# Output projection of the last head but one, moved into the tail of the last head

## The chip, the cores and the metric

The kernel runs on one core of a Trainium2 chip. TensorE (PE) multiplies and writes to PSUM; PEld is its weight load. VectorE (DVE), ScalarE (ACT) and GpSimd (POOL) do the element-wise work, SyncE (SP) issues most transfers, and POOL issues transfers that add to what is in SBUF. The metric is the device time of one execution in microseconds (us), lower is better. The profile shows one execution.

## The reference

One inference step of a two-layer decoder in fp32: 512 prompt tokens and 8 x 4 sample tokens (544 columns), model width 1024. Each layer is a mixer and a gated FFN. Layer 0 mixes by a short convolution, layer 1 by retention with 4 heads. What matters here is the retention mixer and the swiglu behind it:

```python
def swiglu(x, w_gate, w_up, w_down):
    return (jax.nn.silu(x @ w_gate) * (x @ w_up)) @ w_down
...
    z = x @ w_in
    q, k, v, g = jnp.split(z, [QK_DIM, 2 * QK_DIM, 2 * QK_DIM + V_DIM], axis=-1)
...
    o, S = retention_chunkwise(q, k, v, s0)
    of = o.astype(jnp.float32)
    mu = jnp.mean(of, axis=-1, keepdims=True)
    var = jnp.mean(jnp.square(of - mu), axis=-1, keepdims=True)
    of = (of - mu) * lax.rsqrt(var + GN_EPS)
    of = of.transpose(0, 2, 1, 3).reshape(B, L, V_DIM) * gn_g.astype(jnp.float32)
    out = (jax.nn.silu(g) * of.astype(x.dtype)) @ w_out
...
        x = x + m
        x = x + swiglu(rmsnorm(x, norm_ffn[i]), ffn_w_gate[i], ffn_w_up[i], ffn_w_down[i])
```

`retention_chunkwise` gives, per head, causal scores within the new tokens, the part that comes from the state `s0`, and the new state. The sample tokens have a state per sequence of 256 x 512 per head (read and written), the prompt starts at zero.

## The kernel before

**Products.** Activations are held transposed: `x[k]` is a 128 x 544 tile of 128 model features, in two halves of 272 columns. Every fp32 operand is split into a high and a low part (`xh`, `xl`; `wh`, `wl`), and a product is three passes: high x high, high x low, low x high. `project` (L165-180) does this for one 128-column block of weights: per k-tile three passes over two halves, so 48 matmuls for 8 k-tiles and 24 for 4. `split` (L187-190) makes the parts: ACT copies the high part, DVE subtracts. `split_adding` (L192-196) makes the low part without DVE: ACT copies twice and POOL issues a load that adds the weights in memory onto the negated high part. `load_piece` (L133) loads a weight block on SP (`w`) and splits it; `w`, `wh` and `wl` have three buffers each. `residual` (L265-271) adds a product from PSUM to `x` on DVE.

**PSUM.** `psum()` gives a wide tile of two banks, tag `mm`, of which there are two; `bank()` gives single banks, tag `sm`, four of them. A new tile waits until the readers of the old tile in its buffer are done. `wide(...)` (L66) sets which kinds `psum()` takes in turn.

**Order.** The program is written for the engines together; a planner in the framework orders each engine's queue, and `tc.issue_after` pins some instructions behind others. Tiles of one tag share buffers in turn.

**Stages.** The convolution mixer, FFN 0 (from about 155 us), the retention mixer head by head (L1166-1231), FFN 1 (from about 1080 us), the final norm. The FFN's gate and up products use a scheme of seven products for eight blocks: `weights7` (L424) forms sums of weight blocks on DVE, `operand` (L573) forms sums of blocks of `x`, and a `Job` runs `product` 1 to 7 (`sm` banks, matmuls at L476). `run` (L511) calls `prepare` (weights of a job), then `begin`, `middle` and `end`, and prepares the next job ahead of `middle`. The gate's `Silu` is at L598. `start` runs one activation of `Copy` at L302 early on, the "warm" one.

**One head.** `value` (L885) projects the values from four weight pieces (`rtv`), and in its middle splits the rotated queries and keys (`qk_split`, L878), forms the sample scores and transposes the keys. Then come four gate projections (`gate_project`, L994: 48 matmuls, DVE multiplies by the norm, ACT applies Silu and a scale), the prompt's state (L958) and the scores (L1010). The tail interleaves, for the four blocks of 128 prompt tokens and the four sample states:

- `sample_outputs` (L1100): products of sample queries and a state S; `i` = 0 begins with L1106,
- `states_update` (L1113): four matmuls at L1124 into two wide tiles, DVE adds them to S in two halves (L1129), SP stores S (L1130); `states_load` (L1095) loads the next S on SP,
- `inner` (L1042): the scores times values for one token block,
- `normalized` (L1030): statistics on DVE (L1035, L1036), a power on POOL (L223), `yn` on DVE (L1039),
- `gated` (L1059): four transposes of `yn` on PE, and DVE multiplies the gate tile by them (L1066, for the sample tokens L1070).

In heads 0 to 2 the query and key projections of the next head lie among these steps. Then `out_project` (L1132) splits the head's gated output (`yh`, `yl`) and runs eight pieces n = 0 to 7 of 24 matmuls, each with an addition to `x[n]`; the next head follows. In the last head, gate projections 2 and 3 lie in the tail instead, and `out_project` gets `rest`: the left half of pieces 0 and 1 first, before the last block is gated, then the right half; its weights but the first are split by `split_adding`.

Of the kernel before, what the change touches and what calls it, by code (L numbers as in the profile page):

```python
# [47 lines left out]
def hybrid_decode_kernel(ctx: ExitStack, tc: tile.TileContext, a: dict, o: dict):  # L48
# [226 lines left out]
    with ExitStack() as c0:  # L275
# [13 lines left out]
        def start():  # L289
# [221 lines left out]
    def run(jobs, after, steps):  # L511

        jobs[0].lead = True
        jobs[0].prepare()
        jobs[0].begin()
        jobs[0].weave = jobs[1].weave = steps
        for i, job in enumerate(jobs):
            nxt = jobs[i + 1] if i + 1 < len(jobs) else None
            if nxt is not None:
                nxt.prepare()  # L520
            job.middle()
            if nxt is not None:
                nxt.begin()
            job.end()
            after(i)
# [19 lines left out]
    def ffn(layer, next_gain):  # L545
        with ExitStack() as c1:
# [86 lines left out]
            def down(ms, order):  # L633
# [36 lines left out]
            groups = [list(range(m, min(m + GROUP, HJ))) for m in range(0, HJ, GROUP)]  # L670
            jobs = [job for m in range(HJ) for job in gate_up(m)]

# [101 lines left out]
    with ExitStack() as c2:  # L774
# [103 lines left out]
        def qk_split(h, st, which):  # L878
            r = st["rot"][which]
            th = tp.tile([P, 2, SEQ], F32R, tag=f"qkh{which}", name=nm("qkh"), bufs=1)  # L880
            tl = tp.tile([P, 2, SEQ], F32R, tag=f"qkl{which}", name=nm("qkl"), bufs=1)
            split(th, tl, r[:, :, :SEQ])
            st["qk"[which]] = (th, tl)
# [109 lines left out]

        def gate_project(h, st, n, inside=None):  # L994
            if n == 0:
                st["gate"] = tp.tile([P, 4, T], F32, tag="gate", name=nm("gate"), bufs=1)
            wh, wl = load_piece(a["rtg"][h, n], KT * P)
            pt = [bank(), bank()] if inside else psum()
            if inside:
                project(pt, wh, wl, 0, xh, xl, last=False, ks=range(KP))  # L1000
                inside()
                project(pt, wh, wl, 0, xh, xl, first=False, ks=range(KP, KT))
            else:
                project(pt, wh, wl, 0, xh, xl)
            g = halves(st["gate"][:, n, :])
# [53 lines left out]
        def gated(h, st, yn, it, pt=None):  # L1059

            pt = bank() if pt is None else pt
            for n in range(4):
                last_product[0] = nc.tensor.transpose(pt[:, token_tiles(n)], yn[:, token_tiles(n)], ident)
            if it < 4:
                gs = st["gate"][:, :, token_tiles(it)]
                nc.vector.tensor_mul(gs, gs, pt.rearrange("p (n t) -> p n t", n=4))  # L1066
            else:
                gs = st["gate"][:, :, SEQ:].rearrange("p n (g c) -> p n g c", g=4)
                ys = pt.rearrange("p (n g c) -> p n g c", n=4, g=4)[:, :, :, 0:8]
                nc.vector.tensor_mul(gs, gs, ys)  # L1070

# [59 lines left out]

        def out_project(h, st, rest=None):  # L1132
# [6 lines left out]
            def split_gated(c):  # L1139
                for n in range(4):  # L1140
                    split(yh[n][:, c], yl[n][:, c], st["gate"][:, n, c])

            split_gated(slice(0, HT if rest else T))
            wide("m" if rest else "mms")
            for n2 in (0, 2, 1, 3):
                wh, wl = load_piece(a["rtout"][h, n2], 2 * 4 * P, adding=rest is not None and n2 > 0)
                pts = []
                for n in range(2):
                    pts.append(psum())
                    if n2 == 0 and rest:  # L1150
                        rest[n]()
                        project(pts[n], wh, wl, n * 4 * P, yh, yl, hfs=(0,))
                    else:
                        project(pts[n], wh, wl, n * 4 * P, yh, yl)
                        residual(2 * n2 + n, pts[n])
                if n2 == 0 and rest:
                    split_gated(slice(HT, T))
                    for n in range(2):
                        project(pts[n], wh, wl, n * 4 * P, yh, yl, hfs=(1,))
                        residual(n, pts[n])  # L1160
            wide("m")

# [3 lines left out]
        for h in range(NH):  # L1166
# [24 lines left out]
            if more:  # L1191
                nxt = qk_start(h + 1)
                for which in (1, 0):
                    qk_scale(nxt, which)
                with tc.issue_after(last_product[0].ins):
                    qk_project(h + 1, nxt, 1, 0)
                with tc.issue_after(last_product[0].ins):
                    gated_pair(h, st, (yn0, 0), (yn1, 1))
                sample_outputs(h, st, 3)
                p3 = inner(h, st, 3)  # L1200
                yn2 = normalized(p2)
                yns = normalized(st["po"])
                states_update(h, st, 2)

                def inside():
                    states_update(h, st, 3)
                    gated(h, st, yn2, 2)

                qk_project(h + 1, nxt, 1, 1, inside)
                yn3 = normalized(p3)  # L1210
                gated_pair(h, st, (yns, 4), (yn3, 3))
# [3 lines left out]
            else:  # L1215
                yn2 = normalized(p2, "gt")
                gate_project(h, st, 2, lambda: states_update(h, st, 2))

                def inside():
                    sample_outputs(h, st, 3)  # L1220
                    states_update(h, st, 3)

                gate_project(h, st, 3, inside)
                yns = normalized(st["po"], "rot1")
                gated_pair(h, st, (yn0, 0), (yn1, 1))
                gated(h, st, yn2, 2)
                p3 = inner(h, st, 3)
                gated(h, st, yns, 4)
                yn3 = normalized(p3)
                out_project(h, st, [lambda: None, lambda: gated(h, st, yn3, 3)])  # L1230
            st = nxt
    ffn(1, None)


# [114 lines left out]
```

## Time and profile before

| what | value |
|---|---|
| median of 3 runs | 1468.25 us (1466.82 to 1468.54) |
| profiled execution | 1468.62 us, span 1466.40 us |
| mean granted PE clock | 0.996 |
| PE busy | 1449.5 us, 99% of the span |
| DVE busy | 959.4 us, 65% |
| ACT busy | 632.1 us, 43% |
| POOL busy | 130.5 us, 9% |

Times inside the profile count from the span's start. A matmul's record overlaps the next one's, so the spacing of starts, not the length of a record, is what one costs. The chain is followed back from the last instruction to whatever released each step. A stretch's row gives the busy time of each engine in it and the clock that the throttle granted to PE, as a share of full speed: a PE that is busy at clock 0.5 does half the work.

### The profile page before, as it was taken

The page shows a single profiled execution, that of the slowest core. Times are in us where ns is not written, and L with a number is a line of the kernel's source. Part 1 is how long each engine was busy: PE and PEld are TensorE (multiplying, and loading weights), DVE is VectorE, ACT ScalarE, POOL GpSimd, SP SyncE. Part 2 cuts the span into 40 slices and gives each one's busy share as a digit, 9 for nine tenths or more (in the row PEclk, how much of TensorE's full clock was granted, in tenths as well). Part 3 has the DMA queues.
Part 4 walks back from the last instruction along what each step waited for, and adds up shares of the span by engine and source line. Part 5 has one row for each costly group of instructions (what it writes and reads, how often), then busy time and mean ns, then how long its engine had stood idle before and what let it go on. Part 6 is the DMA issues. An engine that isn't in the chain of part 4 may idle for free.

```text
span 1466.4 us, 26224 instructions
## 1 busy us (share of the span) xinstructions
PE 1449.5 (99%) x10920; PEld 1378.7 (94%) x10920; DVE 959.4 (65%) x1489; ACT 632.1 (43%) x925; POOL 130.5 (9%) x171
## 2 busy tenths in 40 slices
PE   9999999999999999999999999999999999999997
PEld 9999999999999999898988978987789999999997
DVE  5644678848748557648546835835698847748655
ACT  5222467626536435241141223214286626526434
POOL 0100011101101003000000000000111101101002
PEclk9999999999999999999999999999999999999999
DMA  6222246635536436237234623713646635536432
GB/s 225 78 95 89 89 104 146 153 109 130 130 108 149 125 73 199 92 115 258 75 124 164 202 81 112 253 53 120 202 113 140 146 115 129 143 106 140 122 80 83
DMA packets 80694, 189.62 MB, mean 129 GB/s; under 512 B 7728, under 2 KB 25008, under 8 KB 80576
## 3 DMA queue, kind: packets, MB, share of 16 engines
q1 hardware_dynamic: 66576, 162.01, 35.2%
q0 software_dynamic: 13136, 24.72, 10.3%
q8 instruction: 85, 1.39, 0.4%
q10 hardware_dynamic: 864, 1.22, 0.2%
q14 instruction: 33, 0.27, 0.1%
HBM read 166.75 MB, written 21.18 MB: 128 GB/s over the span
## 4 chain that ended last, share of the span: by engine, by line
PE 90%; DVE 6%; DMA 1%; ACT 1%; POOL 1%; issue 1%; DVEq 0%; POOLq 0%; ACTq 0%
PE mm L173 37%; PE sm L476 31%; PE sm L173 8%; PE sm L897 2%; PE sm L898 2%; PE sm L899 2%; PE sm L161 1%; PE sm L163 1%; PE sm L162 1%; PE sm L1108 1%; DVE S L1129 1%; DMA w<-in_ffgu_dram 1%; DVE ol L189 1%; DVE wl L189 1%; DMA S<-in_rets_dram 1%
## 5 line engine op out<-in xcount | busy, mean ns | idle before, releaser
L188 ACT ACTIVATE wh<-w 128x1024 fp32r<-128x1024 f32 (+4 forms) x139 | 129.6, 936 | 346.6 <-PE mm L173 223.3
L476 PE MATMUL sm<-oh,wh 128*128 128x272 f32 x704 | 204.2, 290 | 3.1 <-ACT oh L188 1.7
L476 PE MATMUL sm<-ol,wh 128*128 128x272 f32 x704 | 203.5, 289 | 1.1 <-DVE ol L189 1.1
L476 PE MATMUL sm<-oh,wl 128*128 128x272 f32 x704 | 203.3, 289 | 0.2 <-DVE wl L420 0.2
L173 PE MATMUL mm<-xh,wh 128*128 128x272 f32 x932 | 195.3, 290 | 0.0
L173 PE MATMUL mm<-xh,wl 128*128 128x272 f32 x932 | 192.5, 289 | 0.0
L173 PE MATMUL mm<-xl,wh 128*128 128x272 f32 x932 | 192.4, 288 | 0.0
L189 DVE TENSOR_TENSOR wl<-w,wh 128x1024 fp32r<-128x1024 f32 (+4 forms) x139 | 150.2, 1085 | 27.7 <-ACT wh L188 25.4
L269 DVE TENSOR_TENSOR x<-x,mm 128x544 f32<-128x544 f32 x91 | 65.4, 719 | 139.1 <-PE mm L173 139.0
L476 PE MATMUL sm<-oh,h 128*128 128x272 f32 x528 | 152.0, 288 | 0.0
L476 PE MATMUL sm<-oh,l 128*128 128x272 f32 x528 | 151.7, 288 | 0.0
L476 PE MATMUL sm<-ol,h 128*128 128x272 f32 x528 | 151.6, 287 | 0.0
L173 PEld LDWEIGHTS mm<-xh,wh 128*128 128x128 f32 x932 | 146.5, 189 | 4.8 <-DVE wl L189 3.4
L173 PEld LDWEIGHTS mm<-xl,wh 128*128 128x128 f32 x932 | 146.2, 189 | 0.1
L173 PEld LDWEIGHTS mm<-xh,wl 128*128 128x128 f32 x932 | 145.5, 189 | 0.2
L476 PEld LDWEIGHTS sm<-oh,wh 128*128 128x128 f32 x704 | 132.7, 188 | 4.6 <-ACT oh L188 2.3
L476 PEld LDWEIGHTS sm<-ol,wh 128*128 128x128 f32 x704 | 132.8, 189 | 1.5 <-DVE ol L189 1.5
L476 PEld LDWEIGHTS sm<-oh,wl 128*128 128x128 f32 x704 | 133.5, 190 | 0.5 <-DVE wl L420 0.5
L422 POOL DMA_DIRECT2D wl<-in_ffgu_dram x88 | 75.5, 858 | 647.9 <-ACT wl L421 298.3
L419 ACT ACTIVATE wh<-w 128x1024 fp32r<-128x1024 f32 x88 | 93.3, 1060 | 75.0 <-PE sm L476 47.9
L476 PEld LDWEIGHTS sm<-oh,h 128*128 128x128 f32 x528 | 99.4, 188 | 0.2 <-ACT oh L188 0.2
L476 PEld LDWEIGHTS sm<-oh,l 128*128 128x128 f32 x528 | 99.6, 189 | 0.0
(260 smaller groups left out, 3087.3 us busy)
## 6 DMA issues: line engine op xcount, KB each, us to landing
w<-in_ffgu_dram SPq DMA_DIRECT2D x88, 512.0 KB, 4.0
wl<-in_ffgu_dram POOLq DMA_DIRECT2D x88, 256.0 KB, 4.7
w<-in_ffdn_dram SPq DMA_DIRECT2D x96, 192.0 KB, 2.6
S<-in_rets_dram SPq DMA_DIRECT2D x16, 1024.0 KB, 7.6
out_rets_dram<-S SPq DMA_DIRECT2D x16, 1024.0 KB, 5.5
w<-in_cvin_dram SPq DMA_DIRECT2D x21, 512.0 KB, 3.5
w<-in_rtqk_dram SPq DMA_DIRECT2D x16, 512.0 KB, 3.6
w<-in_rtv_dram SPq DMA_DIRECT2D x16, 512.0 KB, 3.6
```

Source lines behind the costliest of these rows:

```text
L161: nc.tensor.matmul(out, lh, rh, start=start, stop=False, skip_group_check=True)
L162: nc.tensor.matmul(out, lh, rl, start=False, stop=False, skip_group_check=True)
L173: last_product[0] = nc.tensor.matmul(half(pt, hf)[:, :HT], w[:, c], act[k][:, hf * HT : (hf + 1) * HT], start=(first and k == ks[0] and i ...
L188: h = nc.scalar.activation(dh, src, AF.Copy)
L189: last_low[0] = nc.vector.tensor_sub(dl, src, dh.bitcast(F32))
L269: last_residual[0] = nc.vector.tensor_add(xk, xk, p)
L419: nc.scalar.activation(wh, w, AF.Copy)
L422: nc.gpsimd.dma_start(wl[:, n:], src[:, n:], accum_op=ALU.add)
L476: last = nc.tensor.matmul(out, w[:, c], b[k][:, at, :], start=(first and k == 0 and i == 0), stop=(k == n - 1 and i == 2), skip_group_chec ...
L897: nc.tensor.matmul(out, xh[kt][:, ts_], wh[:, cw], start=(kt == 0), stop=False)
L898: nc.tensor.matmul(out, xh[kt][:, ts_], wl[:, cw], start=False, stop=False)
L899: nc.tensor.matmul(out, xl[kt][:, ts_], wh[:, cw], start=False, stop=(kt == KT - 1))
```

## The change

- The warm activation is `Silu` instead of `Copy`.
- In both FFNs the jobs are made, and the first one's weights prepared, ahead of the loop that forms the operands.
- `qk_split` puts high and low parts into one tile (tag `qkhl0`, `qkhl1`).
- The last head's gates lie in two tiles of two blocks each (in the buffers of `gt` and `qkhl1`), so the gate tile of head 2 stays alive. `gated` works per tile: two DVE multiplies in the last head where there was one.
- Head 2 no longer runs `out_project`. In the last head, once all gates are projected (as in the other heads, ahead of the first `sample_outputs`), `held_parts` splits head 2's gated output into `xh[0..3]` and `xl[0..3]`, which held x until then. `held_project(n)` is one piece of head 2's output projection with its addition to x. Pieces 4, 5, 2 and 3 stand in the tail where other heads have the next head's query and key projections; piece 5 in single banks.
- Pieces 0, 1 and, later, 6 and 7 of head 2 stay in PSUM without an addition (`held[n]`), and `last_project` adds the last head's product on top of them before one addition to x. Its order is 0, 1, 4, 5, 2, 3, 6, 7; the split by halves (`rest`) is gone; all its weights but the first are made by `split_adding`.

```diff
-                nc.scalar.activation(warm, ones[:, 0:1], AF.Copy)
+                nc.scalar.activation(warm, ones[:, 0:1], AF.Silu)
...
         jobs[0].lead = True
-        jobs[0].prepare()
         jobs[0].begin()
...
+            jobs = [job for m in range(HJ) for job in gate_up(m)]
+            jobs[0].prepare()
             made_in = MADE if layer == 0 else list(range(KT))
...
+            if h == NH - 1 and n % 2 == 0:
+
+                t = tp.tile([P, 2, T], F32, tag=("gt", "qkhl1")[n // 2], name=nm("gate"), bufs=1)
+                st["gate"].append(t)
...
+        def gated_parts(st):
             yhh = vp.tile([P, 4, T], F32R, tag="vyh", name=nm("yh"), bufs=1)
             yll = vp.tile([P, 4, T], F32R, tag="vyl", name=nm("yl"), bufs=1)
             yh = [yhh[:, n, :] for n in range(4)]
             yl = [yll[:, n, :] for n in range(4)]
...
+            for n in range(4):
+                split(yh[n], yl[n], gate_tile(st, n))
+            return yh, yl
...
+        held = {}
+
+        def held_parts(st):
+            for n in range(4):
+                split(xh[n], xl[n], gate_tile(st, n))
+
+        def held_project(n, add=True, single=False):
+
+            if n % 2 == 0:
+                held["w"] = load_piece(a["rtout"][NH - 2, n // 2], 2 * 4 * P)
+            pt = [bank(), bank()] if single else psum()
+            project(pt, *held["w"], n % 2 * 4 * P, xh[:4], xl[:4], last=add)
+            if add:
+                residual(n, pt)
+            else:
+                held[n] = pt
+
+        def last_project(st):
+            y = gated_parts(st)
+            ws = {}
+            for n in (0, 1, 4, 5, 2, 3, 6, 7):
+                if n >= 6:
+                    held_project(n, False)
+                if n % 2 == 0:
+                    w = load_piece(a["rtout"][NH - 1, n // 2], 2 * 4 * P, adding=n > 0)
+                pt = held[n] if n in held else psum()
+                project(pt, *w, n % 2 * 4 * P, *y, first=n not in held)
+                residual(n, pt)
...
-            if more:
-                gate_project(h, st, 2)
-                gate_project(h, st, 3)
+            gate_project(h, st, 2)
+            gate_project(h, st, 3)
+            if not more:
+                held_parts(older)
             sample_outputs(h, st, 0)
...
+            if more:
                 qk_project(h + 1, nxt, 1, 1, inside)
+            else:
+                held_project(5, single=True)
+                inside()
+                held_project(2)
+            yn3 = normalized(p3)
+            if not more:
+                held_project(3)
+            gated_pair(h, st, (yns, 4), (yn3, 3))
+            if more:
                 qk_project(h + 1, nxt, 0, 0)
                 qk_project(h + 1, nxt, 0, 1)
+            if h < NH - 2:
                 out_project(h, st)
...
+            elif not more:
+                held_project(0, False)
+                held_project(1, False)
+                last_project(st)
```

The removed `else` branch held the last head's own order: gate 2 around `states_update` 2, gate 3 around `sample_outputs` 3 and `states_update` 3, then the transposes and `out_project` with `rest`.

More of the change, by code (lines that the diff above doesn't have):

```diff
@@ L1137, in out_project @@
             yl = [yll[:, n, :] for n in range(4)]
[L1139 to L1144, printed above, removed]
+            for n in range(4):
+                split(yh[n], yl[n], gate_tile(st, n))
+            return yh, yl
+        def out_project(h, st):
+            y = gated_parts(st)
+            wide("mms")
             for n2 in (0, 2, 1, 3):
-                wh, wl = load_piece(a["rtout"][h, n2], 2 * 4 * P, adding=rest is not None and n2 > 0)
-                pts = []
+                w = load_piece(a["rtout"][h, n2], 2 * 4 * P)
@@ L1148, in out_project @@
                 for n in range(2):
[L1149 to L1160, printed above, removed]
@@ L1203, in hybrid_decode_kernel @@
[L1203 to L1207, printed above, removed]
[L1209 to L1211 removed]
+                else:
+                    held_project(4)
+            with tc.issue_after(last_product[0].ins):
+                gated_pair(h, st, (yn0, 0), (yn1, 1))
+            sample_outputs(h, st, 3)
@@ L1212, in hybrid_decode_kernel @@
+            gated_pair(h, st, (yns, 4), (yn3, 3))
+            if more:
                 qk_project(h + 1, nxt, 0, 0)
                 qk_project(h + 1, nxt, 0, 1)
+            if h < NH - 2:
                 out_project(h, st)
[L1215 to L1230, printed above, removed]
```

64 lines of the change are left out of this document (35 added, 29 removed).

## The prediction

> **What bounds the kernel now.** I read the page's engine totals first, then the share of each engine in the chain that ended last, then the busy time of each engine by stage (stretch, its length, then busy time of PE, PEld, DVE, ACT and POOL, then the granted clock).
>
> ```profile
> PE 1449.5 (99%) x10920; PEld 1378.7 (94%) x10920; DVE 959.4 (65%) x1489; ACT 632.1 (43%) x925; POOL 130.5 (9%) x171
> ...
> PE 90%; DVE 6%; DMA 1%; ACT 1%; POOL 1%; issue 1%; DVEq 0%; POOLq 0%; ACTq 0%
> ```
>
> ```profile
> 897.00:1005.00 108.00, 107.93 (x744) 93.01 (x743) 65.39 (x99) 27.21 (x35) 3.24 (x5) 1.00 0.42 142
> 1005.00:1105.00 100.00, 94.71 (x660) 83.53 (x660) 75.98 (x131) 53.43 (x84) 11.12 (x14) 0.97 0.53 144
> ```
>
> PE is busy 99% of the span and makes 90% of the chain, so the change, which moves matmuls without adding or removing any, can win only PE's idle time and its slow clock. The stretch from 897 holds head 2, its output projection and the start of head 3: PE idles 0.07 us there. The next holds the rest of head 3 and the entry of the second FFN: PE idles 100 - 94.71 = 5.29 us and the clock averages 0.97. This is what PE waited for there (wait, count, longest), and where it lost time:
>
> ```profile
> PE sm L476 <- ACT oh L188: 1.7, 1, 1.7
> PE mm L173 <- ACT yh L188: 1.2, 1, 1.2
> PE sm L476 <- DVE ol L189: 0.8, 1, 0.8
> PE sm L161 <- DVE yn L1039: 0.4, 1, 0.4
> ```
>
> ```profile
> 1050.00:1052.00 2.00, 1.61 (x12) 1.19 (x10) 2.00 (x4) 0.00 (x0) 0.00 (x0) 1.00 0.90 239
> 1052.00:1054.00 2.00, 1.17 (x7) 0.99 (x8) 1.49 (x6) 1.39 (x4) 0.73 (x1) 1.00 0.81 156
> 1054.00:1056.00 2.00, 1.75 (x10) 1.53 (x9) 1.58 (x4) 0.00 (x0) 0.00 (x0) 0.64 0.54 107
> 1056.00:1058.00 2.00, 2.00 (x11) 2.00 (x11) 0.46 (x1) 0.00 (x0) 0.00 (x0) 0.51 0.00 0
> ...
> 1082.00:1084.00 2.00, 0.54 (x3) 0.30 (x2) 2.00 (x4) 0.87 (x2) 0.00 (x0) 1.00 0.00 0
> 1084.00:1086.00 2.00, 0.68 (x2) 0.42 (x3) 2.00 (x5) 1.40 (x2) 0.14 (x1) 0.82 0.00 0
> 1086.00:1088.00 2.00, 2.00 (x10) 2.00 (x11) 2.00 (x3) 0.98 (x2) 0.71 (x1) 0.50 0.56 133
> 1088.00:1090.00 2.00, 2.00 (x15) 2.00 (x15) 2.00 (x5) 0.85 (x3) 0.00 (x0) 0.83 0.97 236
> ```
>
> Idle is followed by a slow clock. Busy time times what the clock lacked: 1.75 x 0.36 + 2 x 0.49 = 1.6 us at 1054-1058, and 0.68 x 0.18 + 2 x 0.50 + 2 x 0.17 = 1.5 us at 1084-1090. So this stretch loses 5.3 + 3.1 = 8.4 us: nearly all at two places, the output projection's start (its operand's split on ACT) and the FFN's entry (DVE busy throughout, operands late).
>
> A third place lies in the first FFN:
>
> ```profile
> 221.41 1.28 ACT L598 ACT_TABLE_LOAD   x1
> ```
>
> ```profile
> 224.00:226.00 2.00, 1.16 (x10) 0.95 (x9) 2.00 (x3) 1.97 (x4) 0.27 (x1) 1.00 0.07 23
> ```
>
> ACT loads a table, and 0.84 us of PE idle follows, with no slow clock after it. All losses: 8.4 + 0.84 = **9.2 us**, the most that can be won.
>
> **The change, part by part.** The sum is made against the profiled execution: 1468.62 us, its span 1466.40 and 2.22 around it. That is 0.37 above the median of 1468.25, to which I take the result over.
>
> *Warm activation as Silu.* In the built order the load at L598 is gone and the one at the start stays, so the 0.84 us can go. Two ACT operations, not the load alone, stand between the load and PE's next weights; 1.28 off ACT exceeds 0.84, so I take all of it (bounds 0 and 0.84).
>
> *First job's weights prepared ahead of the operand loop.* In the first FFN this shifts a few DVE operations by one or two places around a gap in which DVE waits for a load:
>
> ```profile
> 196.02 0.69 DVE L435 TENSOR_TENSOR w<-w,w 128x512 f32<-128x512 f32 x1 [2.71 <-DMA w<-in_ffgu_dram]
> ```
>
> Two moved operations of 0.7 fit in 2.71: nothing (1.4 without the gap). In the second FFN it counts, below.
>
> *Out-projection of head 2 taken from ahead of head 3.* PE goes from the last query matmuls straight into `value(3)`. What the 24 us covered is the rotation of the queries on DVE and the loads of the value weights.
>
> ```profile
> 949.84 0.72 DVE L865 TENSOR_TENSOR rot<-mm,gt 128x544 f32<-128x544 f32 x1
> ...
> 953.65 0.72 DVE L876 TENSOR_TENSOR rot<-rot,rt 128x544 f32<-128x544 f32 x1
> ```
>
> ```profile
> 973.70 0.39 PE L897 MATMUL sm<-wh,xh 128*128 128x512 f32 x1
> ```
>
> The rotation ends at 954.4. PE would reach its first user 11 us after 949.6 (from 973.70 two weight pieces take until 985), at about 960.9: nothing lost; with that cover gone it would be 4.8. On SP the four value loads take the places of four `rtout` loads; those move behind gates 2 and 3, ahead of the last stores. Nothing lost.
>
> *Gates in two tiles, `held_parts`.* Each gated multiply becomes two halves: 5 more DVE operations, about 0.1 us each beyond the halved width, off PE's path. The eight split operations, 4 on ACT and 4 on DVE of about 0.7 us, lie under gate 3's 6 us and are read 8.8 us after it: nothing.
>
> *Head 3's tail.* The inner products' waits are now filled with held pieces. I time it from T, the start of the first sample output (L1106), with head 2's rows, where the same steps run in this order around a 48-matmul query projection.
>
> ```profile
> 908.98 0.39 PE L1106 MATMUL sm<-vs,scp 128*128 128x512 f32 x1
> ...
> 917.75 0.41 PE L173 MATMUL mm<-xh,wh 128*128 128x272 f32 x2
> ...
> 923.72 0.60 PE L1063 MATMUL mm<-cb,yn 128*128 128x128 f32 x4
> ...
> 925.88 1.04 PE L1108 MATMUL sm<-S,qm 128*8 128x512 f32 x8
> ...
> 928.69 0.51 PE L1124 MATMUL mm<-vs,kns 32*128 32x512 f32 x4
> ```
>
> ```profile
> 913.53 4.30 SPq L1130 DMA_DIRECT2D out_rets_dram<-S  x2
> ...
> 919.72 3.70 SPq L1098 DMA_DIRECT2D S<-in_rets_dram  x2
> ```
>
> ```profile
> S<-in_rets_dram SPq DMA_DIRECT2D x1, 1024.0 KB, 5.9
> ```
>
> ```profile
> S<-in_rets_dram SPq DMA_DIRECT2D x1, 1024.0 KB, 8.6
> ```
>
> Held 4 starts at T+8.8 and, as half of the 5.97 from 917.75 to 923.72, ends at T+11.8. From there to update 2 is 928.69 - 923.72 = 4.97, less sample 3's 0.98, which now comes later: T+15.8. After 0.44 for the update and one matmul, sample 3 is wanted at T+16.35. Its state is loaded at 919.72, T+10.74, and lands 5.9 to 8.6 later (the row of this load, and the slowest): T+16.6 to T+19.3. Wait **0.3** (0 to 3.0; I take this load's own row). Then sample 3, the rest of held 5 (23 x 0.125 = 2.9), update 3 and four transposes: held 2 is wanted at T+21.4. It needs one of the two wide PSUM buffers, which the first half of state update 3 on DVE frees:
>
> ```profile
> 929.46 1.21 DVE L1129 SCALAR_TENSOR_TENSOR S<-S,mm 128x1024 f32<-128x1024 f32 x1
> 930.59 0.80 DVE L1039 TENSOR_SCALAR yn<-sm,mv,rs 128x512 f32<-128x512 f32 x1
> ```
>
> ```profile
> 1027.00 1.42 DVE L1035 BATCH_NORM_STATS2 bst<-sm 128x6 f32<-128x512 f32 x2
> ...
> 1033.30 0.15 DVE L222 TENSOR_SCALAR rs<-mv 128x1 f32<-128x1 f32 x1
> 1034.18 0.81 DVE L1039 TENSOR_SCALAR yn<-sm,mv,rs 128x512 f32<-128x512 f32 x1 [0.72 <-POOL rs L223]
> ```
>
> DVE, in the built order: update 2 starts 0.77 after its matmuls, T+16.55; two halves at 1.13 each (929.46 to 930.59), T+18.8; two statistics, 1.35; small ones, 0.3; 0.88 from `rs` to `yn` by way of POOL; `yn` 0.72; two gate halves 0.7; half of update 3, 1.13: T+23.9. PE waits **2.5** there (0.6 if the statistics, the turn over POOL and the gate halves, 1.9 in all, overlap better; 3.0 at most). Later, held 0 waits for an addition to x: 0.72 less the four transposes ahead of it, **0.5** (0 to 0.7).
>
> *Slow clock.* 1.22 us of idle in 1050-1054 (0.39 + 0.83) was followed by the rates 0.64 and 0.51; 0.84 at 224 was not. A wait of 2.5 is nearer the first: a dip at **1.6**, as at 1054 (0 to 3.1, two dips). [...]
>
> *Start of the last projection.* Head 3's own split, on which PE waited 1.2, now lies under held 0 and 1 (6 us). What is late next is the low part of the weights of pieces 6 and 7. Their buffers come free 4 pieces of 3.01 us after the start of the last projection, P+12.0; two ACT copies and two operations of the FFN's squares ahead of them end at P+14.1 to P+15.8; POOL issues 0.3 later; the landing took
>
> ```profile
> wl<-in_rtout_dram POOLq DMA_DIRECT2D x3, 512.0 KB, 7.0
> ```
>
> ```profile
> wl<-in_rtout_dram POOLq DMA_DIRECT2D x1, 512.0 KB, 5.6
> ```
>
> so P+20.0 to P+23.1, and PE asks at 7 x 3.01 + 0.3 = P+21.4. I take P+22.1, with ACT late and between the landings' ends: **0.7** (0 to 1.7). The earlier pieces have 3 to 4 us to spare.
>
> *Entry of the second FFN.* Four additions to x fall away (1, 0, 6, 7 no longer twice), and the first job's weights are prepared ahead of later operands.
>
> ```profile
> 1060.91 0.72 DVE L269 TENSOR_TENSOR x<-x,mm 128x544 f32<-128x544 f32 x1
> ...
> 1080.52 0.71 DVE L269 TENSOR_TENSOR x<-x,mm 128x544 f32<-128x544 f32 x1
> ```
>
> Before, 19.6 us lay between the first and the last addition for DVE's operand work, which then ran on to 1096 while PE starved. After, pieces 6 and 7 are double: 9 x 3.01 = 27 us of PE for about 26 of DVE, by the built order's operations at their durations. The last operand chain is just in time: **0.3** (0 to 4.9, all that is lost there now with its dip).
>
> **Sum.** New losses: 0.3 + 2.5 + 0.5 + 1.6 + 0.7 + 0.3 = 5.9. Gain 9.2 - 5.9 = 3.3 from 1468.25: **1465.0 us**.
>
> **Rivals.**
> 1. The wait comes without a slow clock: gain 4.9, 1463.4; with DVE running better too, waits of 1 in all, 1460. For it: 0.84 us cost no clock. Against: 1.22 did.
> 2. Little measurable: the state load takes 8.6 (wait 3.0 for 0.3) or a second dip of 1.5 comes; gain 0.6 to 1.8, 1466.5 to 1467.7. For it: the slow landing is in the trace. Against: this load's own row.
> 3. Slower: DVE's service of the two wide PSUM buffers becomes the bound. Each piece of 3.01 us needs one, freed by an addition of 0.72 queued behind state updates of 1.21 and statistics. If five of the ten pieces wait 1.5 (7.5) and two dips follow (3.1) with the 1.8 of other waits, the losses are 12.4: 1471.5. It decides once new losses pass 9.2. Against: DVE's 75.98 busy of 100 leaves room.
>
> **Numbers.** Forecast (1464 to 1466.5) 0.40, of which I put half beyond 0.2%; rival 1 0.30; rival 2 0.12; rival 3 0.18. 0.2% is 2.94 us, about what a measurement of this kernel can tell from no change. Faster: 0.20 + 0.30 = 0.50; same 0.20 + 0.12 = 0.32; slower 0.18. The range 1459.5 to 1471 leaves out half of rival 3 and more, and the last bit of rival 1. The cases of a gain alone: 1459.5 to 1466.5.
>
> **What would show it.** No table load at L598 and PE full at 224. PE's waits from 1005 on: a wide PSUM buffer freed by L1129 around held 2, about 2.5; the accumulated `wl` ahead of pieces 6 and 7, under 2; no 1.7 on `oh` and no clock below 1 at the FFN's entry. I am wrong if PE still idles over 2 us at the entry (DVE work not covered), if `value(3)` waits, or if several PSUM waits on x additions add up.

## The result, and the profile after

The changed kernel takes 1461.33 us (median of 6 runs, 1460.43 to 1463.54) where the kernel before took 1467.74 beside it (6 runs, 1466.82 to 1468.54). The ratio is 0.996, with a 95% interval of 0.9947 to 0.9973: 4.0 to 7.8 us faster. The forecast was 3.3 us faster; the direction and the range hold, the gain is about twice the forecast.

The page of the changed kernel, engine totals and share of the chain:

```profile
PE 1444.1 (99%) x10920; PEld 1374.5 (94%) x10920; DVE 956.2 (66%) x1483; ACT 631.3 (43%) x920; POOL 130.5 (9%) x171
...
PE 92%; DVE 5%; ACT 1%; DMA 1%; POOL 1%; issue 0%; DVEq 0%; SPq 0%; ACTq 0%; POOLq 0%
```

The profiled execution took 1460.43 us, span 1458.4. PE does the same 10920 matmuls in 5.4 us less busy time: busy time contains the slow clock (in the kernel before, 128x272 matmuls start 0.125 us apart at clock 1.00, from 1053.54 to 1054.04, and 0.23 apart at 0.5, from 1055.51 to 1056.87: a little over half the work). By stage (columns as in the prediction; head 2 to the start of the last head's gates, then the tail and the FFN's entry), and the stretches of the tail and the entry in which PE idles:

```profile
897.00:997.00 100.00, 99.93 (x656) 83.55 (x655) 59.57 (x90) 28.53 (x39) 3.24 (x5) 1.00 0.45 151
997.00:1100.00 103.00, 99.28 (x757) 90.94 (x756) 80.09 (x136) 53.91 (x77) 12.03 (x15) 1.00 0.53 143
```

```profile
1024.00:1028.00 4.00, 3.24 (x24) 1.79 (x24) 3.32 (x4) 0.00 (x0) 0.00 (x0) 1.00 0.19 71
1028.00:1032.00 4.00, 2.96 (x24) 2.33 (x23) 3.42 (x10) 1.06 (x1) 1.05 (x2) 1.00 0.69 259
...
1080.00:1084.00 4.00, 2.62 (x19) 2.19 (x18) 4.00 (x8) 2.77 (x6) 0.45 (x1) 1.00 0.54 90
```

Idle in the tail and the entry is 103 - 99.28 = 3.7 us where it was 5.3, and the granted clock is 1.00 throughout, where 3.1 us had gone to a slow clock.

Where the time went can be read from the starts of the FFN's groups of products (L476), between which both kernels run the same number of matmuls. In the first FFN, from its first product to its second group, it is 126.54 us before and 125.20 now. From the last group of the first FFN to the first product of the second, with all of the retention mixer between, it is 553.46 and 550.57. In the second FFN, from its first product to its second group, it is 130.11 and 126.49. These are 1.3, 2.9 and 3.6 us; with 0.2 at the start they are the 8.0 us between the two spans.

What PE waited for from 980 to 1105:

```profile
PE mm L173 <- DVE S L1137: 1.0, 1, 1.0
PE sm L476 <- ACT g L535: 0.9, 1, 0.9
PE sm L1116 <- DMA S<-in_rets_dram: 0.8, 1, 0.8
PE sm L476 <- ACT oh L188: 0.5, 1, 0.5
PE mm L173 <- ACT wh L194: 0.5, 1, 0.5
```

The first is the wait of held piece 2 for the wide buffer, the third the state load ahead of sample output 3 (L1108 before, L1116 now): both were forecast, with other sizes. The last is held piece 0. The copy named is for a later piece, and PE does not read it there: DVE's addition to `x` for piece 3, at 1038.19, which frees the wide buffer that held piece 0 takes, ran to 1038.91, and PE went on at 1039.06. The two with L476 are the FFN's entry.

### The profile page after: what moved, and what is told of

The parts are those of the page before. It is cut to its first block, busy times and chain, and to the rows that moved or that the text cites. A ratio compares the mean times of both kernels' runs of the same rounds, so it can differ in the third digit from the quotient of the medians.

```text
span 1458.4 us, 26223 instructions
## 1 busy us (share of the span) xinstructions
PE 1444.1 (99%) x10920; PEld 1374.5 (94%) x10920; DVE 956.2 (66%) x1483; ACT 631.3 (43%) x920; POOL 130.5 (9%) x171
## 3 DMA queue, kind: packets, MB, share of 16 engines
q0 software_dynamic: 13136, 24.72, 10.2%
q10 hardware_dynamic: 864, 1.22, 0.2%
## 4 chain that ended last, share of the span: by engine, by line
PE 92%; DVE 5%; ACT 1%; DMA 1%; POOL 1%; issue 0%; DVEq 0%; SPq 0%; ACTq 0%; POOLq 0%
PE mm L173 39%; PE sm L476 31%; PE sm L173 7%; PE sm L897 2%; PE sm L898 2%; PE sm L899 2%; PE sm L161 2%; PE sm L163 1%; PE sm L162 1%; DVE S L1137 1%; PE sm L1116 1%; PE mm L904 1%; DVE wl L189 0%; DVE x L269 0%; PE mm L1068 0%
## 5 line engine op out<-in xcount | busy, mean ns | idle before, releaser
L173 PE MATMUL mm<-xh,wh 128*128 128x272 f32 x1020 | 213.1, 290 | 1.6 <-DVE S L1137 1.0
L173 PE MATMUL mm<-xh,wl 128*128 128x272 f32 x1020 | 210.7, 289 | 0.0
L173 PE MATMUL mm<-xl,wh 128*128 128x272 f32 x1020 | 210.0, 287 | 0.1
L476 PE MATMUL sm<-oh,wh 128*128 128x272 f32 x704 | 203.4, 289 | 1.1 <-ACT g L535 0.9
L476 PE MATMUL sm<-ol,wh 128*128 128x272 f32 x704 | 202.8, 288 | 0.0
L476 PE MATMUL sm<-oh,wl 128*128 128x272 f32 x704 | 202.4, 288 | 0.0
L173 PEld LDWEIGHTS mm<-xh,wh 128*128 128x128 f32 x1020 | 159.9, 188 | 7.3 <-DVE wl L189 3.4
L173 PEld LDWEIGHTS mm<-xl,wh 128*128 128x128 f32 x1020 | 159.6, 188 | 0.3 <-DVE xl L201 0.3
L173 PEld LDWEIGHTS mm<-xh,wl 128*128 128x128 f32 x1020 | 159.0, 188 | 0.2
L476 PE MATMUL sm<-oh,h 128*128 128x272 f32 x528 | 152.2, 288 | 0.5 <-ACT oh L188 0.5
L476 PE MATMUL sm<-oh,l 128*128 128x272 f32 x528 | 151.6, 288 | 0.0
L476 PE MATMUL sm<-ol,h 128*128 128x272 f32 x528 | 151.6, 287 | 0.0
L476 PEld LDWEIGHTS sm<-oh,wh 128*128 128x128 f32 x704 | 132.2, 188 | 1.9 <-ACT g L535 1.5
L476 PEld LDWEIGHTS sm<-oh,wl 128*128 128x128 f32 x704 | 132.8, 189 | 0.0
L476 PEld LDWEIGHTS sm<-ol,wh 128*128 128x128 f32 x704 | 132.2, 188 | 0.2 <-DVE ol L189 0.2
L476 PEld LDWEIGHTS sm<-oh,h 128*128 128x128 f32 x528 | 99.4, 188 | 1.1 <-ACT oh L188 0.9
L476 PEld LDWEIGHTS sm<-oh,l 128*128 128x128 f32 x528 | 99.4, 188 | 0.0
```

Source lines behind the costliest of these rows:

```text
L173: last_product[0] = nc.tensor.matmul(half(pt, hf)[:, :HT], w[:, c], act[k][:, hf * HT : (hf + 1) * HT], start=(first and k == ks[0] and i ...
L476: last = nc.tensor.matmul(out, w[:, c], b[k][:, at, :], start=(first and k == 0 and i == 0), stop=(k == n - 1 and i == 2), skip_group_chec ...
```

## Experiments

All ratios are to the kernel before, run beside each on the same chip; the changed kernel has 0.996.

### The warm activation alone

```diff
-                nc.scalar.activation(warm, ones[:, 0:1], AF.Copy)
+                nc.scalar.activation(warm, ones[:, 0:1], AF.Silu)
```

(on the kernel before)

> The kernel before with the warm activation as Silu and nothing else. Theory: the table load in the first FFN goes, and with it the wait of 0.8 us that followed it (the prediction's 0.84): about 1466.9. Rival: between the first FFN's first product and its second group of products the changed kernel took 125.20 us against 126.54, so the load costs more than the wait shown, 1.3 to 1.5 us: about 1466.3. Second rival: what that stretch won came from the early weight preparation, and this kernel stays at 1467.7.

Measured: 1467.32 us, ratio 0.9993 (0.9984 to 1.0001): 1.0 us faster, with an interval from 2.4 faster to 0.2 slower. The trace is clearer than the time. PE at 224 to 226 in this kernel, where it had 1.16 of 2 us and now has all:

```profile
224.00:226.00 2.00, 2.00 (x18) 2.00 (x18) 2.00 (x5) 1.25 (x3) 0.85 (x1) 1.00 0.21 70
```

The wait goes; whether the load is worth 0.8 or 1.4 us the times don't tell. The trace does: from the first product of the first FFN to its second group this kernel takes 125.12 us where the kernel before takes 126.54, so 1.4 us, as the rival had it. This run showed something else, by chance. Around the start of the last output projection it has the same wait as the kernel before, and no slow clock behind it:

```profile
1050.00:1054.00 4.00, 2.56 (x17) 1.90 (x15) 3.48 (x9) 1.39 (x4) 0.73 (x1) 1.00 0.77 156
1054.00:1058.00 4.00, 3.72 (x26) 3.29 (x27) 2.73 (x7) 1.39 (x4) 0.00 (x0) 1.00 0.16 31
```

1.44 us of idle, then clock 1.00; the kernel before had 1.22 us of idle there and then 0.64 and 0.51. The same wait in the same code is followed by a slow clock in one execution and not in another. At the entry of the second FFN it was the other way round: there this execution spent 6.8 us at half clock, and the kernel before 3.4.

### The early weight preparation alone, and the changed kernel without it

```diff
         jobs[0].lead = True
-        jobs[0].prepare()
         jobs[0].begin()
...
+            jobs = [job for m in range(HJ) for job in gate_up(m)]
+            jobs[0].prepare()
             made_in = MADE if layer == 0 else list(range(KT))
```

(on the kernel before; and, the other way round, undone in the changed kernel)

> The kernel before with the first job's weights prepared ahead of the operand loop, in both FFNs, and nothing else. Theory: at the second FFN's entry DVE stays the bound, since the work is only reordered; between 0.5 us slower and 1 us faster. Rival: the early weights are the main gain at that entry; about 3 us faster, 1464.7, with PE's waits at 1080 to 1090 gone.

> The changed kernel with the first job's weights prepared inside run, as before. Theory: the entry of the second FFN is covered by the double pieces 6 and 7 and by the four additions less, so it costs under 1 us: 1461.3 to 1462.3. Rival: early weights carry that entry: about 3 us slower, 1464.3, with a wait of over 2 us and a slow clock there.

Alone on the kernel before: 1473.66 us, ratio 1.0033 (1.0021 to 1.0046), 4.8 us **slower**, which neither theory had. Undone in the changed kernel: 1462.04 us, ratio 0.996 (0.9946 to 0.9973), the same as with it. So the early preparation is no part of the gain of the changed kernel. Alone it does nothing in the first FFN (126.43 us from the first product to the second group, for 126.54); the loss is at the entry of the second, 137.18 for 130.11. The profiled execution is the slowest of the five, at a mean clock of 0.992 where the others have 0.993 to 0.997. Two of PE's waits there, and two stretches:

```profile
PE sm L476 <- DVE ol L189: 1.7, 2, 1.2
...
PE sm L476 <- DVE wl L420: 1.0, 1, 1.0
```

```profile
1088.00:1092.00 4.00, 1.57 (x8) 1.15 (x8) 3.98 (x8) 1.92 (x3) 0.00 (x0) 1.00 0.38 66
1092.00:1106.00 14.00, 13.31 (x61) 12.87 (x60) 5.92 (x11) 4.60 (x10) 2.43 (x2) 0.51 0.32 94
```

DVE is full until 1092 and PE idles 2.4 us: sums of the first job's weights (L436 at 1088.40, L437 at 1090.28) stand in DVE's queue between the low parts of operands (`ol`) that PE waits for, and PE then waits for the low part of those weights (`wl`) as well. Then PE runs at half clock for 14 us, although it hardly waits any more. The slow clock costs more (0.49 x 13.31 = 6.5 us) than the wait that precedes it.

### Held pieces added by themselves

```diff
-                    held_project(n, False)
+                    held_project(n)
...
-                held_project(0, False)
-                held_project(1, False)
+                held_project(0)
+                held_project(1)
```

(on the changed kernel: both edits, then the second alone for pieces 0 and 1, then the first alone for 6 and 7; the matmuls stay the same, and each piece is one more addition to x)

> The changed kernel with pieces 0, 1, 6 and 7 of head 2 added to x by themselves, not held in PSUM: four additions of 0.72 us more on DVE, the same matmuls. Theory: DVE is busy throughout ahead of the second FFN's first product, so what it gets more there PE waits longer: the two additions of pieces 6 and 7 count (1.4 us), those of 0 and 1 lie where DVE is half idle: 1 to 3 us slower, 1462.3 to 1464.3. Rival: DVE catches up: within 0.5 us of the changed kernel. Second rival: the wide PSUM buffers, which must be emptied between the two products of each piece, add waits ahead of the last project too: over 4 us slower.

> The changed kernel with pieces 0 and 1 of head 2 added to x by themselves; 6 and 7 stay in PSUM. Adding all four by themselves cost 6.3 us (1467.68 for 1461.33). Theory: the second FFN's entry is where DVE is the bound and its small waits bring a slow clock behind them; pieces 0 and 1 are added 25 us earlier, where DVE has gaps, so at most 1.5 us: 1461.3 to 1462.8, no clock below 1 at the entry. Rival: the sum of DVE's work counts wherever it is, half of the 6.3: about 1464.5.

> The changed kernel with pieces 6 and 7 of head 2 added to x by themselves; 0 and 1 stay in PSUM. Theory: these two additions (1.4 us of DVE) stand in the queue right ahead of the second FFN's first operands and carry nearly all of the 6.3 us: 1465 to 1468, with half clock of 7 to 11 us behind the entry in the trace. Rival: half, 1464.5, without a slow clock.

Measured: all four 1467.68 us, 0.9996 (0.9987 to 1.0004); 0 and 1 alone 1462.42, 0.9958 (0.9944 to 0.9972); 6 and 7 alone 1467.44, 0.9992 (0.9983 to 1.0001). With all four added by themselves no gain is left that can be measured; that is more than the theory's 1 to 3 us and has the size of the second rival, but not its mechanism, since the waits ahead of the last projection are as in the changed kernel (0.9, 0.9 and 0.5 for 1.0, 0.8 and 0.5). Pieces 0 and 1 cost nothing that can be measured. Pieces 6 and 7, two additions of 0.72 us, carry the whole: 0.0032 of 1468, 4.7 us. In the traces that is in one place: from the first product of the second FFN to its second group 131.61 us with 6 and 7 added by themselves, for 126.49 in the changed kernel; the other two stages differ by 0.2 and 0.4. And it is not the chance of one execution: the mean granted clock is 0.994 to 0.996 in all 11 executions with 6 and 7 added by themselves, and 0.997 to 0.999 in all six of the changed kernel. The waits of the kernel with 6 and 7 added by themselves, and the stretches around the FFN's entry:

```profile
PE sm L476 <- DVE wl L420: 1.3, 1, 1.3
PE mm L173 <- DVE S L1137: 1.1, 1, 1.1
PE sm L476 <- DVE ol L189: 0.8, 1, 0.8
```

```profile
1082.00:1086.00 4.00, 1.52 (x9) 0.87 (x7) 4.00 (x8) 3.66 (x5) 0.00 (x0) 1.00 0.26 45
1086.00:1096.00 10.00, 10.00 (x56) 9.92 (x56) 4.46 (x9) 2.45 (x6) 2.43 (x2) 0.66 0.48 131
```

1.44 us more on a DVE that is full there make PE's idle 2.5 us in four (in the changed kernel 1.4), and a stretch at clock 0.66 over 10 us follows, 3.4 us lost. In the kernel with all four:

```profile
1078.00:1087.00 9.00, 6.13 (x39) 4.98 (x39) 9.00 (x16) 7.45 (x12) 0.85 (x1) 1.00 0.47 86
1087.00:1097.00 10.00, 10.00 (x46) 9.92 (x47) 4.17 (x8) 1.46 (x4) 2.43 (x2) 0.52 0.48 131
```

2.9 us of idle over nine, then 10 us at 0.52. These kernels still have the early preparation, which by itself did harm at a DVE-bound entry. What the two additions would cost without it was not tried.

### A longer wait at held piece 2

```diff
+                more_ops = 1 if h == NH - 1 and i == 3 and w == 0 else 0
-                nc.vector.scalar_tensor_tensor(Si, Si, _gamma(h) ** 4, pu, op0=ALU.mult, op1=ALU.add)
+                nc.vector.scalar_tensor_tensor(Si, Si, _gamma(h) ** 4 / 2**more_ops, pu, op0=ALU.mult, op1=ALU.add)
+                for _ in range(more_ops):
+                    nc.vector.scalar_tensor_tensor(Si, Si, 2.0, pu, op0=ALU.mult, op1=ALU.subtract)
```

(on the changed kernel, with 1 and with 2)

> The changed kernel with state update 3 of the last head made in two steps on its first half, which frees the wide PSUM buffer for held piece 2 by 1.1 us later: the wait of 1.04 us there becomes 2.2 (the prediction had 2.5). The prediction's step: such a wait brings a stretch of slow clock that costs 1.6, so 2.7 us slower in all, 1464.0. Rival: the wait alone counts, with the clock at 1: 1462.4.

> The same with three steps on the first half: the wait becomes 3.3 us. The prediction's step: 2.3 for the longer wait and 1.6 for the clock, 1465.2. Rival: no slow clock, 1463.6. Second rival: the slow stretch lasts 10 us as in the run with four additions more, 5 us of clock: 1468.6.

Measured: with one step more 1463.29 us, 0.9964 (0.9951 to 0.9976); with two 1463.78, 0.9969 (0.9959 to 0.9979). Against 0.996 that is 0.6 and 1.3 us, less than the intervals' width. The wait, and the stretch with it and the one behind it, with one step more:

```profile
PE mm L173 <- DVE S L1138: 2.1, 1, 2.1
```

```profile
1030.00:1034.00 4.00, 1.92 (x16) 1.47 (x13) 4.00 (x6) 0.70 (x1) 0.00 (x0) 1.00 0.18 64
1034.00:1038.00 4.00, 4.00 (x34) 4.00 (x33) 3.18 (x6) 0.00 (x0) 0.00 (x0) 1.00 0.86 275
```

A single wait of 2.1 us, 2.08 of idle in four, and the clock stays at 1.00. With two steps the wait came out at 2.2, not at 3.3, since the second step did not lie wholly on PE's path; the clock stayed at 1.00 too. So waits of 2.1 and 2.2 brought no dip in these two executions, which are the fastest of their five and eight; 2.5 itself was not met. Another execution of the second kernel took 1466.42 us at a mean clock of 0.996, where the profiled one has 0.998: it may have had a dip, at a place that is not known.

### Held piece 2 in single banks; the fourth state loaded early

```diff
-                held_project(2)
+                held_project(2, single=True)
```

```diff
+            if h == NH - 1 and i == 3:
+                S = st["S"][i] = tp.tile([P, 4, T], F32, tag="gate", name=nm("S"), bufs=1)[:, :, :DV]
...
                 held_parts(older)
+                states_load(h, st, 3)
```

(each alone on the changed kernel; in the second the load at its old place is left to the other heads)

> The changed kernel with held piece 2 in two single banks in place of a wide PSUM buffer, so that it doesn't wait for state update 3 on DVE. Theory: the 1.04 us wait goes and nothing takes its place: ratio to the kernel before 0.0007 lower than the changed kernel's 0.996. Rival: the single banks are held by outputs that DVE has yet to normalise, so the same wait stands there under another name: 0.996.

> The changed kernel with the last head's fourth state loaded into the tile of head 2's gates, free once its parts are split, so that the load waits for no store. Theory: the 0.76 us wait ahead of sample output 3 goes, but PE then reaches held piece 2 earlier by as much and waits there for the same DVE work: 1.0 becomes up to 1.8, and the time stays (0.996). Rival: the two waits are separate, 0.8 us faster (0.9955).

Measured: single banks 1460.13 us, 0.9945 (0.9931 to 0.9959); early state 1460.52, 0.9949 (0.9937 to 0.9962). Both medians are below the changed kernel's, 2.2 and 1.6 us by ratio, with overlapping intervals. So they are faster than the changed kernel on median, but the traces do not show it: the spans are 1458.7 and 1458.0 us, and the changed kernel's is 1458.4. The two together, without a third edit, were not run. The tail's waits with single banks:

```profile
PE sm L1068 <- DVE yn L1044: 0.4, 1, 0.4
PE sm L1116 <- DMA S<-in_rets_dram: 0.3, 1, 0.3
```

and with the early state:

```profile
PE mm L173 <- DVE S L1140: 0.9, 1, 0.9
```

In the first, the wide buffer's 1.0 is gone, and 0.4 for `yn` has come ahead of the transposes. In the second the load's 0.8 is gone and the buffer's wait is not longer, so the theory of one chain behind both falls: the statistics of the sample outputs (L1040) come earlier too, and DVE starts the last state update at 1029.65 and not at 1030.64 (the tail starts at the same time in both, 1008.7 and 1008.6).

### Squares on POOL

```diff
-                    square_sum(kt, None, add=nc.vector)
+                    square_sum(kt, None, add=nc.vector if layer == 0 else nc.gpsimd)
```

(on the changed kernel; then together with both edits above)

> The changed kernel with the additions of squares ahead of the second FFN on POOL (1.57 us each there) and not on DVE (0.72, six of them, 4.3 us). Theory: DVE is what the first products of that FFN wait for, so its waits there (0.5 and 0.9 us in the changed kernel) go to under 0.5 in all, and where a slow clock came behind them in some executions, it comes no more: 1 to 2 us faster, ratio about 0.995. Rival: the waits that are left come from ACT's own order (a weight copy of 1.06 ahead of the copy that PE waits for): no change, 0.996.

> The three together: held piece 2 in single banks, the fourth state loaded early, the additions of squares on POOL. Theory: with neither the wide buffer nor the load in the way both waits of the tail (1.8 us) go, and the entry's 1.4 besides: 2.5 to 3.2 us faster than the changed kernel, ratio 0.994. Rival: DVE's chain stands behind all of them, and the waits move on to the next buffer: under 1 us.

Measured: alone 1467.39 us, 0.9994 (0.9985 to 1.0002), 5 us slower than the changed kernel; the three together 1464.98, 0.9979 (0.9969 to 0.9989), with the same wait of 4.0 in its trace. Neither theory nor rival had that. DVE got less to do and came out later: its last addition to `x` runs 5.6 us after the second FFN's first product, and 1.3 in the changed kernel. One wait of PE, and rows of ACT, POOL and DVE, of the first of these kernels:

```profile
PE sm L476 <- ACT g L535: 4.0, 1, 4.0
```

```profile
1067.98 0.66 ACT L217 ACTIVATE sqlast<-x 128x544 f32<-128x544 f32 x1 [2.72 <-POOL sqacc L218]
...
1083.49 0.75 ACT L579 ACTIVATE f<-x,vec 128x544 f32<-128x544 f32 x1 [0.60 <-DVE x L269]
1084.15 0.38 ACT L535 ACTIVATE g<-sm 128x272 f32<-128x272 f32 x1
```

```profile
1073.57 2.74 POOL L218 TENSOR_TENSOR sqacc<-sqacc,sqlast 128x544 f32<-128x544 f32 x1 [1.66 <-ACT sqlast L217]
1077.93 1.83 POOL L218 TENSOR_TENSOR sqacc<-sqacc,sqlast 128x544 f32<-128x544 f32 x1 [1.62 <-DVE f L411]
```

```profile
1069.63 1.01 DVE L420 TENSOR_TENSOR wl<-w,wh 128x512 fp32r<-128x512 f32 x1 [1.38 <-ACT wh L419]
...
1078.48 1.59 DVE L413 TENSOR_TENSOR f<-f 128x272 f32<-128x272 f32 x1
...
1082.75 0.71 DVE L269 TENSOR_TENSOR x<-x,mm 128x544 f32<-128x544 f32 x1
```

The squares share one buffer (`sqlast`). ACT waits 2.72 us for POOL to empty it; the next weight copy stands behind that, and DVE waits 1.38 us for the copy. POOL's addition took 2.74 here (1.37 in another instance), and DVE's 128x272 operations beside these additions up to 1.59 where they take 0.43. So DVE's last addition to `x` is late, ACT's next operation waits for it, and the copy that PE needs (`g`, 1084.15) stands behind that operation in ACT's queue. Which weighs more, the buffer or the slower operations, no run separates. In these rows POOL's addition at 1077.93 ends at 1079.76, and DVE's operation beside it at 1080.07, 0.3 us later.

## Why the prediction was right, and by how much not

The direction was forecast, by mechanisms that the runs mostly show; the size was not. PE's waits in the tail are those that the prediction had named, and the FFN's entry was rightly seen as the place where DVE is the bound. The sizes, by its steps:

| step | predicted | measured |
|---|---|---|
| table load goes | gain 0.84 | 1.3 to 1.4 in the traces; as time, alone, 1.0 (-0.2 to 2.4) |
| `value(3)` without cover | 0 | 0.07 us of idle in 897 to 997 |
| early preparation, first FFN | 0 | 0.1 to 0.2 in the traces, one way and the other |
| early preparation, second FFN | no price of its own | alone a loss of 4.8; in the changed kernel 0 |
| state load | 0.3 | 0.76 |
| wide buffer at held 2 | 2.5 | 1.04 |
| held 0 for an addition to x | 0.5 | 0.47 |
| slow clock in the tail | 1.6 | 0 |
| low weights of pieces 6, 7 | 0.7 | 0 (0.2 to 0.4 in three of the experiments) |
| entry of the second FFN | 0.3 | 1.45 (0.52 and 0.93) |
| sum of new losses | 5.9 | 3.7 |

The step that failed is "*Slow clock*: a wait of 2.5 is nearer the first: a dip at 1.6". It was 1.6 of the 2.2 by which the losses were put too high. One wait of the trace with a dip behind it, and one without, were read as a threshold between 0.84 and 1.22 us. The runs show no such threshold in the length of a wait: 1.22 was followed by a slow clock in two traces and, at the same place, not in a third; 2.1 and 2.2 at held 2 were not. What makes the difference the runs do not show (last section). No dip in the tail is what rival 1 had, and the measured time lies by it (1463.4 to 1460).

The second mis-sized term is the wide buffer. These rows of the changed kernel, PE, then DVE, then SP and the load's landing, show why:

```profile
1024.14 0.51 PE L1132 MATMUL mm<-vs,kns 32*128 32x512 f32 x4
1025.73 1.05 PE L1116 MATMUL sm<-S,qm 128*8 128x512 f32 x8 [0.76 <-DMA S<-in_rets_dram]
...
1031.91 0.52 PE L173 MATMUL mm<-xh,wh 128*128 128x272 f32 x2 [1.04 <-DVE S L1137]
```

```profile
1024.68 2.35 DVE L1137 SCALAR_TENSOR_TENSOR S<-S,mm 128x1024 f32<-128x1024 f32 x2 [1.07 <-PE mm L1132]
...
1029.95 0.78 DVE L269 TENSOR_TENSOR x<-x,sm 128x272 f32<-128x272 f32 x2
1030.64 2.35 DVE L1137 SCALAR_TENSOR_TENSOR S<-S,mm 128x1024 f32<-128x1024 f32 x2
1032.90 0.75 DVE L1074 TENSOR_TENSOR gate<-gate,sm 128x256 f32<-128x256 f32 x2
```

```profile
1017.60 0.43 SPq L1106 DMA_DIRECT2D S<-in_rets_dram  x1
```

```profile
S<-in_rets_dram SPq DMA_DIRECT2D x1, 1024.0 KB, 8.1
```

With T near 1008.6, PE came to held 2 at T+22.3 and not at T+21.4. Half of that is the load, which was issued earlier (T+9.0) but took longer (8.1 where 5.9 was taken); the rest are steps a little longer than taken. DVE freed the buffer at T+23.2 and not at T+23.9: update 2 came 0.3 earlier and started 0.54 after its matmuls, not 0.77, and the statistics were quicker. PE 0.9 later and DVE 0.7 earlier both shorten the wait, by 1.5 together. One link was right by luck: the two gate halves, counted with 0.7, came only behind the update (1032.90), and in their place stood the addition of piece 5 to `x`, of the same length (1029.95).

The third is the entry. "The last operand chain is just in time: 0.3" was too small by 1.1, and not for DVE alone:

```profile
1080.66 0.66 ACT L188 ACTIVATE oh<-f 128x544 fp32r<-128x544 f32 x1 [0.42 <-DVE f L413]
...
1082.67 1.06 ACT L188 ACTIVATE h<-w 128x1024 fp32r<-128x1024 f32 x1 [0.81 <-PE sm L476]
1083.64 0.38 ACT L535 ACTIVATE g<-sm 128x272 f32<-128x272 f32 x1
```

The wait of 0.93 is for the copy of a PSUM sum (`g`, 1083.64), which stands on ACT behind a weight copy of 1.06 for the next job. The prediction costed DVE's queue there and not ACT's.

That the sum is no further off than 2.2 us is luck: its errors are 3.8 us too much (wide buffer, slow clock, low weights) and 1.6 too little (state load, entry). The 9.2 us that could be won were those of one execution, too: they hold two slow stretches, and the execution of the warm activation alone had none at the first of these places and a longer one at the second.

The measured new losses give a gain of 9.2 - 3.7 = 5.5, the medians differ by 6.4 and the two profiled executions by 8.2; that of the changed kernel is the fastest of its six. The stages of the traces place the difference, in us:

| stage | before | changed | warm activation alone | early preparation alone | changed, 6 and 7 added by themselves |
|---|---|---|---|---|---|
| first FFN, first product to second group | 126.54 | 125.20 | 125.12 | 126.43 | 125.03 |
| last group of the first FFN to first product of the second | 553.46 | 550.57 | 552.20 | 553.56 | 550.93 |
| second FFN, first product to second group | 130.11 | 126.49 | 131.50 | 137.18 | 131.61 |

The first row is the table load, half a microsecond more than the 0.84 that was counted. In the second, 1.3 of the 2.9 us are not the change's: the warm activation alone does not touch that stage, and its execution gains them by having no slow stretch there. The changed kernel without the early preparation and the one with pieces 0 and 1 added by themselves take 551.75 and 552.22 for that stage, so the tail's own part is between 0 and 1.6. The third is the entry.

The prediction had the right account of where the gain is possible, and a wrong weight in it. It put "four additions fall away" and "double pieces" together as cover for DVE. The runs show that in the changed kernel two of these additions, 6 and 7, decide the entry. With them back no gain can be measured (0.9992); in that trace, of an execution faster than the median, the first two stages keep theirs, and the entry is 5.1 us longer than in the changed kernel and 1.5 longer than before. Part of that may be the early preparation, which is in this kernel too and cost 4.8 us alone. A kernel with these two additions and without the early preparation was not run, so how much they are worth by themselves stays open. What the traces show is that the entry's gain is more than the covered wait: its idle stays short of what a slow clock followed. From the first product of the second FFN to its second group PE waited 1.4 to 1.8 us in the seven traces without a slow stretch there, and 2.6 to 4.6 in the seven with one.

## What to carry to other kernels

In the changed kernel two vector additions of 0.7 us were worth 4.7 us: they stood on a full engine just ahead of a long run of matmuls, and the idle that they made was followed by 7 to 10 us at half clock. Look for work to take off the engine that is full *where PE restarts*, and hold partial sums in PSUM there; the same saving 25 us earlier was worth nothing that could be measured. And cost every engine's queue at such a place: moving DVE's squares to POOL held up ACT by their shared buffer (one wait of 2.72 us), DVE's 128x272 operations took up to 1.59 us beside POOL's where they take 0.43, and the move cost 5 us.

## What the runs showed of the hardware

The slow clock came in stretches of 3.4 us or whole multiples of it. Where a slow stretch could be measured whole, the time lacking, doubled, is its length: 3.4 us twice in the kernel before (2 x (0.36 + 0.49) / 0.5 at 1054 to 1058), 10.2 us in the kernel with four more additions (10 x 0.48 / 0.5 = 9.6, and its end 0.7 behind these rows), 13.7 in the one with the early preparation alone (14 x 0.49 / 0.5), 6.8 with pieces 6 and 7 added by themselves (10 x 0.34 / 0.5). These are 1, 3, 4 and 2 times 3.4. In the kernel before, the trace's records of the granted clock have the two stretches themselves: 3.413 us each, with 1047.89 us of full clock ahead of the first, 27.31 between them and 372.05 behind the second, which are 307, 8 and 109 times 3.413.

PE's idle time in the 3.4 us ahead of the slow stretches, and in some stretches of 4 us behind which the clock stayed at 1.00:

| kernel | stretch, us | PE idle in it, us | half clock behind it, us |
|---|---|---|---|
| squares on POOL | 1080.4 to 1083.8 | 3.22 | 6.8 |
| all three edits | 1080.6 to 1084.0 | 2.66 | 3.4 |
| before | 1081.9 to 1085.3 | 2.56 | 3.4 |
| warm activation alone | 1079.7 to 1083.1 | 2.45 | 6.8 |
| early preparation alone | 1088.7 to 1092.1 | 2.24 | 13.7 |
| two steps more at held 2 | 1030 to 1034 | 2.20 | 0 |
| all four pieces added by themselves | 1084.0 to 1087.4 | 2.08 | 10.2 |
| one step more at held 2 | 1030 to 1034 | 2.08 | 0 |
| 6 and 7 added by themselves | 1083.9 to 1087.3 | 1.56 | 6.8 |
| early preparation alone | 1051.2 to 1054.6 | 1.48 | 3.4 |
| before | 1051.2 to 1054.6 | 1.46 | 3.4 |
| warm activation alone | 1050 to 1054 | 1.44 | 0 |
| 6 and 7 added by themselves | 1028 to 1032 | 1.44 | 0 |
| two steps more at held 2 | 1082 to 1086 | 1.41 | 0 |
| changed | 1080 to 1084 | 1.38 | 0 |

Ahead of a slow stretch PE idled 1.46 to 3.22 us. In the changed kernel the two waits at the entry, 0.52 and 0.93, come to 1.45, of which 1.38 lie in the four from 1080, so they are only just short of that. The 2.08 and 2.20 at held 2, nearly all of it one wait of 2.1 and 2.2, brought no slow clock, so idle time is not all that counts. What else does, and why one stretch lasts 13.7 us while PE is fed (0.69 us of idle in 14), stays open.
